# Decoder layer on one core: none of the down-projection's weight sums in the key/value stage, half of those in the up-projection through accumulating DMAs, and the down stage's activation fetches moved to another queue

## The chip, the cores and the metric

The kernel runs on one core of a Trainium2 chip. The metric is device time in microseconds (us), from the start of the program to its end, median of the runs; less is better. Engines are named as the profile names them: PE multiplies matrices (PEld loads its stationary operand), DVE is the vector engine, ACT the scalar engine, POOL and SP here mainly issue DMAs, each on a queue of its own that it works through in order.

## The reference

One layer is computed, with a sliding-window attention and a gated convolutional MLP, all in fp32, for 512 tokens of width 2048.

```
h = rms_norm(x, g[0]);  m = swa_sink_attention(h, w_in, w_out, sinks, bias_table);  x = x + rms_norm(m, g[1])
h = rms_norm(x, g[2])
u = h @ w_up                                            # 2048 x 11264
c = conv_w[0]*up[:, 0:S] + conv_w[1]*up[:, 1:S+1] + conv_w[2]*up[:, 2:S+2]    # up: u padded in front
gate, val = split(c);   y = (silu(gate) * val) @ w_down   # 5632 x 2048
x = x + rms_norm(y, g[3])
```

## The kernel before

Each fp32 matrix is split into a high part (ACT, line 64, `wh`) and a rest (DVE, line 65, `wl`), and a product is three matmuls (`prod`). A weight block is 128 x 1024 fp32, 512 KB. Split blocks go into a ring of slots (`halves`), from which PE takes them, so that PE can be a few blocks behind the splits.

Stages, in order of time: the **key/value stage** (lines 163 to 235; loop over 16 slices `kt`, each with one block of `wkv` and 24 matmuls of 512 columns, while x and its transpose are loaded); queries and attention; the output projection (`oproj` and what follows it, lines 495 to 528); the **up stage** (`up_pair(f, g)` for f = 4 to 43, line 705 on, a Strassen-like scheme with 7 products of 24 matmuls of 256 columns, so 168 matmuls, for each pair of gate and value blocks; its weight blocks are `bw`, its result goes to DRAM as `hd`); and the **down stage** (line 725 on; seven products over 22 block rows `kp`, with 88 matmuls of 512 columns and more for each four of them).

The down stage needs, beside the weights `wdn`, sums of them. They are made beforehand, in the stages above: `weight_sums(kp, sums)` loads the four blocks of a block row into four buffers `ts` (POOL's queue), adds them in place (four additions on DVE, line 144) and stores the four results to DRAM as `td` (POOL's queue again). There are 22 such block rows: before, 2 are done in the key/value stage, 6 in the output projection, 14 in the up stage. All use four `ts` buffers, so the loads of a block row wait for the stores of the one before. In the down stage `weight_form` loads a block `raw` (from `td` or `wdn`, SP's queue) and splits it; `fetch` brings `hd` back as `hq` tiles.

The order of the instructions on each engine is not that of the code: a scheduler sets it when the program is built, from its own estimate of times, and places a step where it thinks that its operands are ready. On the chip each engine then works through its list in that order. So the additions of `weight_sums` stand among DVE's splits, and where one waits for a load, the splits behind it wait too.

Of the kernel before, what the change touches and what calls it, by code (L numbers as in the profile page):

```python
# [11 lines left out]
F32 = mybir.dt.float32  # L12
F32R = mybir.dt.float32r
AF = mybir.ActivationFunctionType
ALU = mybir.AluOpType
# [3 lines left out]
P = 128  # L19
# [16 lines left out]
NP = NF // 2  # L36
# [5 lines left out]
def trunk(ctx, tc, xT, x, grow, table, onehot, masked, sinks, conv,  # L42
          wkv, wq, wo, wup, wdn, out):
    nc = tc.nc
# [93 lines left out]
    def weight_sums(kp, sums):  # L138
# [4 lines left out]
        for q, o in ((2, 0), (0, 1), (1, 2), (3, 1)):  # L143
            nc.vector.tensor_tensor(t[q], t[q], t[o], ALU.add)  # L144
            nc.gpsimd.dma_start(td[kp, :, q, :], t[q])
            yield

    def step(g, n=1):
        for _ in range(n):
            next(g, None)  # L150

    with ExitStack() as att:
# [9 lines left out]

        with ExitStack() as ph:
            pa = ph.enter_context(pool("pa", 3))
            tsk = ph.enter_context(pool("tsk", 4))

            zero = pa.tile([P, S], F32, name="zero", bufs=1)
            nc.vector.memset(zero, 0.0)
            for _ in range(2):
                mm(bank(7), zero[:, :P], zero, True, True)  # L170
            nc.scalar.activation(zero[:, 0:1], zero[:, 0:1], AF.Copy)
            first = pa.tile([P, KT + S], F32, name="first", bufs=1)
            gc = first[:, :KT]

            def token_half(b, h, ss):
                r = pa.tile([P, 1024], F32, name="xr")
                nc.sync.dma_start(r, x[b * P:(b + 1) * P, h * 1024:(h + 1) * 1024])
                nc.scalar.activation(r, r, AF.Square, accum_out=ss[:, h:h + 1])
                if h == 1:
                    nc.vector.tensor_tensor(ss[:, 0:1], ss[:, 0:1], ss[:, 1:2], ALU.add)  # L180
                    rstd(rc[:, b:b + 1], ss[:, 0:1], D, pa)

            def x_slice(kt, src):
                src = src.rearrange("p (a b) -> p a b", a=NT)
                nc.scalar.activation(ah[:, :, kt, :], src, AF.Copy, scale=gc[:, kt:kt + 1])
                nc.vector.scalar_tensor_tensor(al[:, :, kt, :], src, gc[:, kt:kt + 1],
                                               ah[:, :, kt, :].bitcast(F32), ALU.mult, ALU.subtract)

            pkv = [bank(i) for i in range(8)]
            ss = None  # L190
            for kt in range(KT):
                if kt == 0:
                    for h in range(2):
                        r = first[:, KT:] if h == 0 else pa.tile([P, 512], F32, name="xs")
                        c = KT + h * S
                        nc.sync.dma_start(r if h else first, xT[:, c if h else 0:c + S])
                        if h == 0:
                            w = halves()
                            raw = wraw.tile([P, 1024], F32, name="raw")
                            for c in (slice(0, 512), slice(512, 1024)):  # L200
                                nc.sync.dma_start(raw[:, c], wkv[0, :, c])
                                split(w[0][:, c], w[1][:, c], raw[:, c])
                        x_slice(h, r)
                elif kt % 2 == 0:
                    r = pa.tile([P, 1024], F32, name="xr")
                    nc.sync.dma_start(r, xT[:, KT + kt * S:KT + (kt + 2) * S])
                    for h in range(2):
                        x_slice(kt + h, r[:, h * 512:(h + 1) * 512])
                if kt:
                    w = weights(wkv, kt)  # L210
                if kt == 3:
                    for t, src in ((tb, table), (oh, onehot), (mk, masked)):
                        tc.keep_in_program_order(nc.sync.dma_start(t, src))
                    for e in range(2):
                        nc.sync.dma_start(sink[e * HD:(e + 1) * HD],
                                            sinks[e:e + 1].to_broadcast([HD, 2 * NKV]).rearrange("p (j g) -> p j g", g=2))
                    nc.sync.dma_start(cw, conv)
                if 4 <= kt < 12:
                    if kt % 2 == 0:
                        ss = pa.tile([P, 2], F32, name="ss")  # L220
                    token_half((kt - 4) // 2, kt % 2, ss)
                if kt == 12:
                    nc.scalar.dma_start(rd.rearrange("b p -> p b"), rc)
                    nc.scalar.dma_start(rb, rd.rearrange("b p -> (b p)")[None, :].to_broadcast([P, S]))
                for i in range(4):
                    o3 = pkv[i].rearrange("p (a b) -> p a b", a=NT)
                    prod(o3, cols(w, i), moving(kt), kt == 0, kt == KT - 1)
                if kt in (7, 11):
                    g = weight_sums(kt // 11, tsk)
                if kt >= 7:  # L230
                    step(g, (1, 0, 3, 2)[(kt - 7) % 4])
                for b in range(NT):
                    prod(pkv[4 + b], station(b, kt), wide(w, 1), kt == 0, kt == KT - 1)
            for i in range(4):
                nc.vector.tensor_tensor(kn[:, i, :], pkv[i], rb, ALU.mult)
# [209 lines left out]
    with ExitStack() as op:  # L445
# [49 lines left out]
        def oproj(d, o):  # L495
            for u in range(8):
                w = weights(wo, 8 * d + u)
                for b in range(NT):
                    for k in range(2):
                        kt = 2 * u + k  # L500
                        prod(o[b], station(b, kt), wide(w, k), kt == 0, kt == KT - 1)
                if u % 4 == 0:
                    g = weight_sums(2 * d + u // 4, sums)
                step(g, (1, 0, 2, 3)[u % 4])
            for b in range(NT):
                evac_m(b, d, o[b])
# [9 lines left out]
        for b, bk in enumerate((2, 5, 6, 7)):  # L516
            o = bank(bk)
            for kt in range(KT):
                prod(o, station(b, kt), wide(ws[kt // 2], kt % 2), kt == 0, kt == KT - 1)
                if b > 1:  # L520
                    turn_tok(b - 2, kt, (0, 1, 3, 4))
                if b < 2:
                    if kt == 0:
                        g = weight_sums(6 + b, sums)
                    if kt in (0, 9, 11, 13, 15):
                        step(g)
            evac_m(b, 3, o)
            xn[b] = finish_tok(b)
# [19 lines left out]
    batches = [(g, min(g + GB, NP)) for g in range(0, NP, GB)]  # L548
    hq = {}

    def fetch(m, par, g0, g1, queue=nc.sync):
        t, k0 = next((t, k) for t, k, k1 in hq[m, par] if k <= g0 < k1)
        queue.dma_start(t[:, g0 - k0:g1 - k0, :], hd[m, par, :, g0:g1, :])

    with ExitStack() as us:
        fp = us.enter_context(pool("fp", 1))
# [145 lines left out]
            nc.scalar.activation(uv[:, HALF:], X[:, :HALF], AF.Copy, scale=-1.0)  # L702
            gate(f, (ug, uv))

        kp, idle = 8, iter(())
        for f in range(4, NF):
            i = f - 4
            g = idle
            if kp < NP and i % 5 in (0, 2):
                work = weight_sums(kp, sums)  # L710
                step(work)
                kp += 1
            if i % 5 in (1, 4):
                g = work
            up_pair(f, g)
            step(g)
            if i == 34:
                tsu.close()
                early = ctx.enter_context(pool("early", 1, side="right"))
                hq[1, 0] = [(early.tile([P, 16, HALF], F32, name="hq10"), 0, 16)]  # L720
                for g0, g1 in batches[:4]:
                    fetch(1, 0, g0, g1)
# [13 lines left out]
    small = ctx.enter_context(pool("small3", 4))  # L736
    last = ctx.enter_context(ExitStack())
    hq[0, 0] = [(last.enter_context(pool("hq00", 1)).tile([P, NP, HALF], F32, name="hq00"), 0, NP)]
    for g0, g1 in batches[4:]:
        fetch(1, 0, g0, g1)  # L740
    for q in ((0, 0), (0, 1), (1, 1)):
        for g0, g1 in batches:
            fetch(*q, g0, g1, nc.gpsimd)
    nc.scalar.dma_start(g3, grow[2:3, :].to_broadcast([P, D]))

    XB, ZB = (3, 4, 6, 7), (0, 1, 2, 5)
# [18 lines left out]
    def weight_form(src, kp):  # L765
        raw = raws[kp % 2].tile([P, 1024], F32, name="raw")
        table, q = src
        nc.sync.dma_start(raw, td[kp, :, q, :] if table else wdn[4 * kp + q])
        hi, lo = halves()
        split(hi, lo, raw)  # L770
        return hi, lo
# [5 lines left out]
    def product(o, form, src, fresh, tail=0):  # L777
        kept = []
        for g0, g1 in batches:
            af = act_form(*form, g0, g1)  # L780
            for kp in range(g0, g1):
                wf = weight_form(src, kp)
                if kp >= NP - tail:
                    kept.append((kp, af, g0, wf))
                    continue
                for t in range(2):
                    for e in range(2):
                        multiply(o, kp, af, g0, wf, t, e, fresh)
        return kept
# [135 lines left out]
```

## Time and profile before

| | |
|---|---|
| median of 3 runs | 1944.05 us (1943.37 to 1945.49) |
| the profiled execution: its time | 1946.71 us |
| its span, first to last instruction | 1944.7 us |
| PE busy | 1876.9 us, 97% |
| DVE busy | 1492.8 us, 77% |
| ACT busy | 982.3 us, 51% |
| mean granted clock of PE | 0.982 |

The busy share of PE is high throughout, so what matters is where it is not: idle time of PE, and stretches with a lower granted clock (1.00 is 2.4 GHz, 0.50 is 1.2 GHz). The windows by stage show both.

### The profile page before, as it was taken

The page shows a single profiled execution, that of the slowest core. Times are in us where ns is not written, and L with a number is a line of the kernel's source. Part 1 is how long each engine was busy: PE and PEld are TensorE (multiplying, and loading weights), DVE is VectorE, ACT ScalarE, POOL GpSimd, SP SyncE. Part 2 cuts the span into 40 slices and gives each one's busy share as a digit, 9 for nine tenths or more (in the row PEclk, how much of TensorE's full clock was granted, in tenths as well). Part 3 has the DMA queues.
Part 4 walks back from the last instruction along what each step waited for, and adds up shares of the span by engine and source line. Part 5 has one row for each costly group of instructions (what it writes and reads, how often), then busy time and mean ns, then how long its engine had stood idle before and what let it go on. Part 6 is the DMA issues. An engine that isn't in the chain of part 4 may idle for free.

```text
span 1944.7 us, 30119 instructions
## 1 busy us (share of the span) xinstructions
PE 1876.9 (97%) x11822; PEld 1699.5 (87%) x11822; DVE 1492.8 (77%) x2079; ACT 982.3 (51%) x1566; POOL 106.1 (5%) x202
## 2 busy tenths in 40 slices
PE   8999999999999998999999999999998899999998
PEld 5878888888899998889999999999997688888886
DVE  5458888755688998999998888888886466666875
ACT  4347777632344444444455555555553455545553
POOL 2000000012100111112100000000000000000000
PEclk9999999999999999999999999999999899999999
DMA  9742333589653688788743333433333955576673
GB/s 353 208 139 81 106 113 106 184 311 327 262 182 132 234 289 269 282 298 307 254 131 114 123 123 119 137 109 120 117 119 123 343 191 192 190 237 200 218 259 118
DMA packets 116045, 375.24 MB, mean 193 GB/s; under 512 B 12704, under 2 KB 26240, under 8 KB 113984
## 3 DMA queue, kind: packets, MB, share of 16 engines
q1 hardware_dynamic: 84128, 263.19, 40.7%
q0 software_dynamic: 27744, 100.94, 14.6%
q10 hardware_dynamic: 4032, 9.21, 1.4%
q8 instruction: 92, 1.51, 0.3%
q14 instruction: 49, 0.40, 0.1%
HBM read 300.90 MB, written 72.39 MB: 192 GB/s over the span
## 4 chain that ended last, share of the span: by engine, by line
PE 67%; DMA 15%; issue 9%; DVE 7%; ACT 1%; POOL 1%; SPq 0%; DVEq 0%; ACTq 0%; POOLq 0%
PE b L83 66%; DMA td<-ts 4%; DMA ts<-in_wdn 3%; DVE wl L65 2%; DMA raw<-in_wo 2%; DMA raw<-in_wkv 1%; DMA xr<-in_x 1%; PE b L86 1%; DVE ts L144 1%; ACT wh L64 1%; DMA raw<-in_wq 1%; DMA raw<-td 1%; DMA bw<-in_wup 0%; DMA xs<-in_xT 0%; POOL ts L141 0%
## 5 line engine op out<-in xcount | busy, mean ns | idle before, releaser
L65 DVE TENSOR_TENSOR wl<-raw,wh 128x1024 fp32r<-128x1024 f32 (+1 forms) x371 | 449.1, 1218 | 240.0 <-ACT wh L64 239.3
L64 ACT ACTIVATE wh<-raw 128x1024 fp32r<-128x1024 f32 (+1 forms) x371 | 388.2, 1055 | 479.8 <-PE b L83 272.9
L83 PE MATMUL b<-ah,wl 128*128 128x256 f32 (+1 forms) x1824 | 564.5, 309 | 23.3 <-DVE wl L65 23.2
L83 PE MATMUL b<-ah,wh 128*128 128x256 f32 (+1 forms) x1824 | 570.5, 313 | 12.4 <-ACT wh L64 6.6
L83 PE MATMUL b<-al,wh 128*128 128x256 f32 (+1 forms) x1824 | 562.2, 308 | 0.4 <-DVE al L65 0.4
L83 PEld LDWEIGHTS b<-ah,wl 128*128 128x128 f32 x1824 | 356.4, 195 | 41.8 <-DVE wl L65 26.9
L83 PEld LDWEIGHTS b<-ah,wh 128*128 128x128 f32 x1824 | 356.4, 195 | 27.5 <-ACT wh L64 10.3
L83 PEld LDWEIGHTS b<-al,wh 128*128 128x128 f32 x1824 | 356.7, 196 | 11.1 <-DVE al L65 0.6
L83 PE MATMUL b<-wh 128*128 128x512 f32 x616 | 241.1, 391 | 18.5 <-ACT wh L64 18.0
L83 PE MATMUL b<-wl,wh 128*128 128x512 f32 x616 | 240.8, 391 | 0.5 <-DVE wl L65 0.5
L83 PE MATMUL b<-wh,wl 128*128 128x512 f32 x616 | 240.6, 391 | 0.0
L64 ACT ACTIVATE wh<-bw 128x1024 fp32r<-128x1024 f32 x160 | 167.7, 1055 | 129.7 <-PE b L83 129.7
L65 DVE TENSOR_TENSOR wl<-bw,wh 128x1024 fp32r<-128x1024 f32 x160 | 194.5, 1219 | 9.7 <-ACT wh L64 9.3
L83 PEld LDWEIGHTS b<-wh 128*128 128x128 f32 x616 | 116.3, 189 | 43.4 <-ACT wh L64 18.4
L83 PEld LDWEIGHTS b<-wl,wh 128*128 128x128 f32 x616 | 116.3, 189 | 25.2 <-DVE wl L65 1.0
L144 DVE TENSOR_TENSOR ts<-ts 128x1024 f32<-128x1024 f32 x88 | 107.4, 1220 | 39.3 <-DMA ts<-in_wdn 35.7
L83 PEld LDWEIGHTS b<-wh,wl 128*128 128x128 f32 x616 | 116.2, 189 | 24.1
L83 PE MATMUL b<-wh,ah 128*128 128x512 f32 x320 | 126.9, 397 | 0.0
L83 PE MATMUL b<-wl,ah 128*128 128x512 f32 x320 | 124.9, 390 | 0.2 <-DVE wl L65 0.2
L83 PE MATMUL b<-wh,al 128*128 128x512 f32 x320 | 124.9, 390 | 0.0
L670 ACT ACTIVATE s<-b 128x256 f32<-128x256 f32 x160 | 59.2, 370 | 90.2 <-PE b L83 90.2
L83 PE MATMUL b<-f5h,wl 128*128 128x256 f32 x320 | 90.9, 284 | 2.2 <-DVE wl L65 2.2
(162 smaller groups left out, 3063.7 us busy)
## 6 DMA issues: line engine op xcount, KB each, us to landing
bw<-in_wup SPq DMA_DIRECT2D x160, 512.0 KB, 3.8
ts<-in_wdn POOLq DMA_DIRECT2D x88, 512.0 KB, 7.3
td<-ts POOLq DMA_DIRECT2D x88, 512.0 KB, 5.8
raw<-td SPq DMA_DIRECT2D x88, 512.0 KB, 4.8
raw<-in_wdn SPq DMA_DIRECT2D x66, 512.0 KB, 4.3
raw<-in_wq SPq DMA_DIRECT2D x32, 512.0 KB, 3.5
raw<-in_wo SPq DMA_DIRECT2D x32, 512.0 KB, 4.6
hd<-c SPq DMA_DIRECT2D x44, 256.0 KB, 3.1
```

The costliest lines, as they stand in the source:

```text
L64: nc.scalar.activation(hi, src, AF.Copy)
L65: nc.vector.tensor_tensor(lo, src, hi.bitcast(F32), ALU.subtract)
L83: tc.keep_in_program_order(nc.tensor.matmul(o, l, r, start=start, stop=stop, skip_group_check=more))
L86: tc.keep_in_program_order(nc.tensor.transpose(o, src, ident))
L144: nc.vector.tensor_tensor(t[q], t[q], t[o], ALU.add)
L670: nc.scalar.activation(t, o[:, :HALF], AF.Copy)
```

## The change

In the key/value stage the two block rows of sums are gone; the output projection takes block rows 0 to 5 instead of 2 to 7. The up stage takes 16 instead of 14: of every five pairs the first starts a `weight_sums` as before, the second runs its additions and then calls `queue_sums`, a new function that makes the same four results without DVE: a load, then a second DMA on POOL's queue that adds its source into the buffer (`accum_op=ALU.add`), then the store. In the down stage the fetches of `hq` that POOL's queue issued at its start are put on SP's queue, in the code one for every two weight blocks.

```diff
+    def queue_sums(kp, sums):
+        t = [sums.tile([P, 1024], F32, name="ts") for _ in range(4)]
+        for q, other in ((2, 0), (0, 1), (1, 2), (3, 1)):
+            nc.gpsimd.dma_start(t[q], wdn[4 * kp + q])
+            nc.gpsimd.dma_start(t[q], wdn[4 * kp + other] if q in (0, 2) else t[other], accum_op=ALU.add)
+            nc.gpsimd.dma_start(td[kp, :, q, :], t[q])
...
-            tsk = ph.enter_context(pool("tsk", 4))
...
-                if kt in (7, 11):
-                    g = weight_sums(kt // 11, tsk)
-                if kt >= 7:
-                    step(g, (1, 0, 3, 2)[(kt - 7) % 4])
...
-                    g = weight_sums(2 * d + u // 4, sums)
+                    g = weight_sums(2 * d - 2 + u // 4, sums)
...
-                        g = weight_sums(6 + b, sums)
+                        g = weight_sums(4 + b, sums)
...
-    def fetch(m, par, g0, g1, queue=nc.sync):
+    def fetch(m, par, g0, g1):
...
-        queue.dma_start(t[:, g0 - k0:g1 - k0, :], hd[m, par, :, g0:g1, :])
+        nc.sync.dma_start(t[:, g0 - k0:g1 - k0, :], hd[m, par, :, g0:g1, :])
...
-        kp, idle = 8, iter(())
+        kp = 6
         for f in range(4, NF):
             i = f - 4
-            g = idle
-            if kp < NP and i % 5 in (0, 2):
+            if i % 5 == 0 and kp < NP:
                 work = weight_sums(kp, sums)
                 step(work)
                 kp += 1
-            if i % 5 in (1, 4):
-                g = work
-            up_pair(f, g)
-            step(g)
-            if i == 34:
+            up_pair(f, work if i % 5 == 1 else iter(()))
+            if i % 5 == 1:
+                step(work)
+            if i % 5 == 1 and kp < NP:
+                queue_sums(kp, sums)
+                kp += 1
+            if kp == NP and tsu:
                 tsu.close()
...
-    for g0, g1 in batches[4:]:
-        fetch(1, 0, g0, g1)
-    for q in ((0, 0), (0, 1), (1, 1)):
-        for g0, g1 in batches:
-            fetch(*q, g0, g1, nc.gpsimd)
+    coming = [(1, 0, *g) for g in batches[4:]] + [(*q, *g) for q in ((0, 0), (0, 1), (1, 1)) for g in batches]
...
                 wf = weight_form(src, kp)
+                if coming and kp % 2 == 0:
+                    fetch(*coming.pop(0))
```

What the scheduler makes of it stands in the orders. POOL's queue in the up stage, before: one block row of sums (buffers `ts_6433` to `ts_6436`; `td<-ts` are the stores, which also wait for DVE's additions):

```order
L141 DMA ts_6433<-in_wdn 128x1024
L141 DMA ts_6435<-in_wdn 128x1024
L145 DMA td_89<-ts_5946 128x1024
L141 DMA ts_6434<-in_wdn 128x1024
L141 DMA ts_6436<-in_wdn 128x1024
L145 DMA td_89<-ts_6435 128x1024
L145 DMA td_89<-ts_6433 128x1024
```

The same queue after the change, from the fifth `queue_sums` on (`ts_8831` to `ts_8834`; line 151 loads, line 152 adds, line 153 stores; lines 141 and 145 belong to the `weight_sums` ahead of it):

```order
L151 DMA ts_8833<-in_wdn 128x1024
L145 DMA td_89<-ts_8342 128x1024
L151 DMA ts_8831<-in_wdn 128x1024
L152 DMA ts_8833<-in_wdn 128x1024
L145 DMA td_89<-ts_8344 128x1024
L151 DMA ts_8832<-in_wdn 128x1024
L152 DMA ts_8831<-in_wdn 128x1024
L153 DMA td_89<-ts_8833 128x1024
L151 DMA ts_8834<-in_wdn 128x1024
L152 DMA ts_8832<-ts_8833 128x1024
L153 DMA td_89<-ts_8831 128x1024
L152 DMA ts_8834<-ts_8832 128x1024
```

The store of the last sum follows in the next row but two, behind two loads of the next `weight_sums`. On DVE the additions stood from the 4th pair of the stage to the 16th, four of them for each 0.9 pairs; after the change they stand in eight groups of four, one group for each 2.4 pairs, from the 4th pair's gate to the 21st's (32 additions in 17.4 pairs).

SP's queue at the start of the down stage, before (`hd<-c` are the last results of the up stage, `raw` the weight blocks kp 0, 2, 4, 6 and then 1, 3, 5 and on, `hq10b` the last part of one activation quarter; the other 18 fetches stand on POOL's queue):

```order
L768 DMA raw<-td 128x1024
L576 DMA hd<-c_15413 128x2x256
L768 DMA raw<-td 128x1024 x2
L576 DMA hd<-c_15650 128x2x256
L553 DMA hq10b<-hd 128x1024
L553 DMA hq10b<-hd 128x512
L768 DMA raw<-td 128x1024 x18
```

And after:

```order
L768 DMA raw<-td 128x1024 x2
L555 DMA hq_15683<-hd 128x1024 x2
L578 DMA hd<-c_15646 128x2x256
L555 DMA hq_15683<-hd 128x1024 x3
L555 DMA hq_15683<-hd 128x512
L555 DMA hq10b<-hd 128x1024
L768 DMA raw<-td 128x1024
L555 DMA hq10b<-hd 128x512
L768 DMA raw<-td 128x1024
L555 DMA hq_15675<-hd 128x1024 x5
L555 DMA hq_15675<-hd 128x512
L555 DMA hq_15676<-hd 128x1024 x5
```

All 18 fetches that POOL's queue had are on SP's queue ahead of the seventh weight block, kp 5: the first six ahead of kp 1, the other twelve between kp 3 and kp 5.

## Rows read from the trace of the kernel before

**Rows 1.** Windows, whole core: span; PE, PEld, DVE, ACT, POOL busy (count); clock; DMA share; GB/s.

```profile
0.00:50.00 50.00, 40.52 (x138) 28.27 (x139) 26.44 (x39) 23.92 (x35) 11.16 (x24) 0.93 0.97 355
...
450.00:500.00 50.00, 50.00 (x222) 41.42 (x221) 30.25 (x29) 15.67 (x26) 11.77 (x22) 1.00 0.90 326
...
800.00:850.00 50.00, 44.12 (x337) 43.30 (x336) 44.49 (x49) 20.81 (x30) 9.59 (x18) 0.93 0.81 286
...
1000.00:1050.00 50.00, 50.00 (x419) 50.00 (x419) 43.38 (x48) 26.05 (x37) 0.00 (x0) 1.00 0.39 127
...
1500.00:1550.00 50.00, 33.55 (x134) 27.15 (x135) 22.66 (x19) 17.66 (x18) 8.55 (x17) 0.80 0.94 349
```

**Rows 2.** PE's timeline, key/value stage: its first and its last matmul (start us, us).

```profile
5.64 0.80 PE L83 MATMUL b<-ah,wh 128*128 128x512 f32 x1
...
106.64 0.39 PE L83 MATMUL b<-wh,al 128*128 128x512 f32 x1
```

**Rows 3.** DMA, 0 to 70 us: all packets; then one issue (count, KB, median us to landing).

```profile
DMA packets 7626, 23.43 MB, mean 335 GB/s; under 512 B 1520, under 2 KB 1712, under 8 KB 7622
ts<-in_wdn POOLq DMA_DIRECT2D x8, 512.0 KB, 9.6
```

**Rows 4.** PE's timeline, up stage: the last product (f4h) of pairs f = 4, 19, 20.

```profile
658.75 0.28 PE L83 MATMUL b<-f4h,wh 128*128 128x256 f32 x1
...
1007.61 0.28 PE L83 MATMUL b<-f4h,wh 128*128 128x256 f32 x1
...
1027.77 0.28 PE L83 MATMUL b<-f4h,wh 128*128 128x256 f32 x1
```

**Rows 5.** DVE, 645 to 960 us: the additions (duration min/median/max ns), and its waits (us, times, longest).

```profile
L144 DVE TENSOR_TENSOR ts<-ts x56: 1207/1218/1228, 655.4 to 948.1; 128x1024 f32<-128x1024 f32 x56
...
DVE ts L144 <- DMA ts<-in_wdn: 15.6, 9, 2.9
DVE raw L679 <- DMA bw<-in_wup: 8.5, 4, 3.7
```

**Rows 6.** DMA, 650 to 960 us, up stage with sums.

```profile
DMA packets 27305, 90.22 MB, mean 291 GB/s; under 512 B 2843, under 2 KB 6171, under 8 KB 27281
q0 software_dynamic: 15981, 58.18, 54.4%
td<-ts POOLq DMA_DIRECT2D x56, 512.0 KB, 6.0
ts<-in_wdn POOLq DMA_DIRECT2D x52, 512.0 KB, 6.3
```

**Rows 7.** DMA, 400 to 520 us, output projection with sums.

```profile
DMA packets 10402, 39.99 MB, mean 333 GB/s; under 512 B 1168, under 2 KB 1168, under 8 KB 9883
td<-ts POOLq DMA_DIRECT2D x24, 512.0 KB, 4.6
ts<-in_wdn POOLq DMA_DIRECT2D x23, 512.0 KB, 7.7
```

**Rows 8.** The tile ts, 645 to 960 us: issue duration in ns; us to landing.

```profile
L141 POOL DMA_DIRECT2D ts<-in_wdn x56: 527/532/549, 646.6 to 938.0; - x56
...
DMA to landing us min/median/max: 2.9/6.2/11.4
```

**Rows 9.** Chain that ended last, start of the down stage (start us, us, what); then PE's wait there.

```profile
1503.92 10.88 DMA raw<-td
...
1517.24 27.77 PE b L83 x110
...
PE b L83 <- ACT wh L64: 18.0, 1, 18.0
```

**Rows 10.** Windows of 2.5 us there, columns as in the first group.

```profile
1497.50:1500.00 2.50, 0.48 (x3) 0.06 (x1) 1.44 (x2) 0.00 (x0) 1.01 (x2) 1.00 0.55 186
...
1507.50:1510.00 2.50, 0.00 (x0) 0.00 (x0) 0.00 (x0) 0.00 (x0) 0.53 (x1) 0.50 1.03 415
...
1522.50:1525.00 2.50, 2.50 (x12) 2.02 (x11) 0.00 (x0) 1.04 (x1) 0.54 (x1) 0.97 1.03 411
```

More of the change, by code (lines that the diff above doesn't have):

```diff
@@ L712, in trunk @@
                 kp += 1
-            if i % 5 in (1, 4):
-                g = work
-            up_pair(f, g)
-            step(g)
-            if i == 34:
+            up_pair(f, work if i % 5 == 1 else iter(()))
[5 more added lines that the diff above has]
+            if kp == NP and tsu:
                 tsu.close()
+                tsu = None
                 early = ctx.enter_context(pool("early", 1, side="right"))
```

## Prediction, made before the change was run

> **What bounds the kernel now.** I read the windows first, since PE is busy 97% of the whole span and an average tells little. In [rows 1] the reader is to see where PE's busy time is short of the window or its clock below 1.00: the first 50 us, the up stage while sums are made (44.12 of 50 at a clock of 0.93), and the start of the down stage (33.55 of 50 at 0.80). The output projection makes sums too, with DMA at 0.90, and PE has no gap. After the sums, from 1000 us on, PE is full and DVE has 43.38 of 50.
>
> Three losses of PE follow, each with its cause.
>
> The key/value stage: its 384 matmuls run from 5.64 to 106.64 us [rows 2], 101.0 us. At the spacing of a full window (50 us for 222, so 0.226 us each [rows 1]) they need 383 x 0.226 = 86.6 us. The loss is 14.4 us. DMA is at 0.97 of its time there [rows 1]; 23.43 MB are moved in the first 70 us [rows 3], of which the sums are 8 loads and 8 stores of 0.524 MB, 8.4 MB, more than a third.
>
> The up stage: the last product of pair 4 begins at 658.75, that of pair 19 at 1007.61, that of pair 20 at 1027.77 [rows 4]. A free pair takes 20.16 us; the 15 pairs took 348.9 where 302.4 were needed. The loss is 46.4 us, half of it clock. The cause is DVE: 56 additions of 1.22 us, 68 us, and 24 us in which it stood before loads [rows 5]. A free pair leaves DVE 20.16 - 20.16 x 43.38/50 = 2.67 us, over 15 pairs 40 us. 68 + 24 - 40 = 52, against 46.4 measured: the account is right to about 6 us, and high.
>
> The down stage's start: PE waits 18.0 us for one split, that of the weight block kp 1, issued at 1503.92 and landed 10.88 us later [rows 9], and the clock is at 0.50 in and after the gap [rows 10]: some 21 us.
>
> **The change part by part.**
>
> Key/value stage. 8.4 MB of 23.4 and 8 additions go. What is left, 15 MB, would take 45 us at the 335 GB/s of [rows 3], half of PE's 87, so DMA is no longer late except in the first blocks. Of 14.4 us I leave 3 for these and the first matmuls: **-11**. Bounds: -14 (nothing is late) and -7 (half of the loss lies in the first three blocks, which wait for their own loads).
>
> Output projection. Six block rows as before, only others: 0. The cover is PE's full windows [rows 1]; were it gone, DVE's lag would cost at most what a sum costs in the up stage, 46.4/14 = 3.3 us each, and their number is the same.
>
> Up stage. Two things have to keep pace with PE. First DVE: 32 additions are 39 us, and by its order they stand over 17.4 pairs, where 17.4 x 2.67 = 46 us are free. Waits for loads were 24/14 = 1.7 us a sum; eight sums make 14 us. 39 + 14 - 46 = 7 us lost. The additions come in groups of four, 4.9 us within some 0.7 pairs that have 1.9 us free: 3 us too much in each of 8 groups, 24 us if PE had no blocks in hand, 0 if its ring covers all. I take 9.
>
> Second POOL's queue. Let L be a load, S a store and A an adding DMA, from issue to landing. Following the queue in the order shown: the last addition lands (A); its store (S) frees the buffer for the fourth load of the next `weight_sums`; behind that load stands the store of its first result (S), which frees the buffer for the first load of the next `queue_sums` (L); then its first addition (A), the one that uses it (A), and the last again. With seven issues of 0.53 us [rows 8] the round is 3A + 2S + L + 3.9. DVE's order gives it 2.41 pairs, 48.5 us. With S = 6.0 and L = 6.3 [rows 6] A may be 8.8; with 4.6 and 7.7, at 333 GB/s [rows 7], 9.2. The second is the better row, because a round at that pace moves 20 x 0.524 MB of sums and 2.41 x 2.36 MB of the pairs' own, 334 GB/s. If a round is longer, additions on DVE wait for their loads, the splits behind them wait, and PE with them, seven times.
>
> No row has an adding DMA. Nearest below is the load at 6.3 [rows 6]: a round of 41 us, nothing lost. Nearest above, if everything but the smallest landing of 2.9 us [rows 8] doubles: 2 x 7.7 - 2.9 = 12.5, a round of 58. I take 9.2, the load at this traffic plus one more transfer of its bytes, an estimate: POOL's queue moved 58.18 MB in 54.4% of 310 us [rows 6], 1.5 us for 0.524 MB. That is a round of 48 to 50, and I put down 5 us. Sum: 7 + 9 + 5 = 21 lost instead of 46: **-25**. Bounds: -42 (the round of 41 us and every group of additions covered by the ring), and +39 (the second rival, below).
>
> The Trainium skill has a rule that speaks against this part: "Collectives: The Full Stack", section "The bandwidth ceiling: the fold count and why AG ≠ RS ≠ AR", says that an add in the DMA path needs two source reads on the same ring, so that it moves data at half the rate of a copy. No run here shows it. By it, if it applied only to the transfer, the sum stays as above; if to all of the time under load, it is the second rival's.
>
> The early fetch of `hq` on SP's queue waits for all sums. Its place is behind the weight loads of pair 25, and the sums end some two pairs after DVE's last addition (3A + 2S + 3 = 40 us by the same walk), near pair 23: 0. Queued behind it are the weights of pairs 26 and on; it would cost PE only with rounds so long that the second rival has them priced.
>
> Down stage. In the code a fetch comes with every second weight block; in SP's order it doesn't. Six fetches of hq_15683 and one of hq10b stand ahead of kp 1, twelve more between kp 3 and kp 5. Kp 1: from 1497 to 1504 some 3.6 MB are issued on one queue and at the 415 GB/s of [rows 10] 2.9 MB of it are moved, so kp 1 has 0.7 and its own 0.5 MB to wait for, and lands near 1510 instead of 1514.8: -5. Kp 5: 6.3 MB behind kp 3, 15 us, lands near 1528, split by 1530; PE, with kp 1 to 4 done, wants it near 1526: +4, and perhaps 2 of clock. **0**, between -8 and +8.
>
> **Sum.** -11 - 25 + 0 = -36. The profiled execution has a span of 1944.7 us and a time of 1946.71, 0.14% over the median of 1944.05; the differences are taken from the median: **1908**.
>
> **The rivals.**
>
> The gain of the up stage is eaten: adding DMAs take about 10.7 us, the round is 53 us, 4.5 x 7 = 31 more are lost, 16 + 31 = 47, what was lost before. Only the key/value stage is left: 1933. For it: landings of 7.7 to 9.6 us at the same traffic [rows 3, 7]. Against it: additions between two buffers don't read DRAM.
>
> Slower, by one mechanism: the queue of POOL is the bound of the up stage, because an adding DMA occupies the DMA engines twice. A = 12.5, a round of 58.3 us against 48.5, 9.8 x 7 = 69 on top of 16: 85 us lost, 39 more than before; less 11, **1972**. It decides from A = 11.2 on, where the total is nought: 16 + 7 x 3 x (A - 9.2) = 46 + 11. For it: the round is a chain of six landings, and nothing of it overlaps. Against it: the 1.5 us of transfer in a landing of 6 to 8 us.
>
> The change doesn't do what it says: the fetches stand together in SP's order. This is certain already and costs 0, as above; its bad end, kp 5 late and the clock down for longer, is +8: 1916, which lies in the forecast's range.
>
> **How the numbers follow.** The forecast (1890 to 1920) has 0.50, the first rival 0.20 for a faster end (1920 to 1940) and 0.05 for one within 0.2% (3.9 us, about what a measurement can tell from no change), the second rival 0.22, better than 1890 0.03. Faster 0.73, same 0.05, slower 0.22. The range has the first rival and the second to just over its price, and leaves out some 0.1 above (A beyond 12.7) and little below: 1885 to 1975.
>
> **What would show it.** Right: the key/value stage's last matmul near 96 us; the pairs from 4 to 21 near 21.3 us each; adding DMAs landing in 8 to 10 us; DVE's waits for `ts` loads below 20 us in the up stage; kp 1 landing earlier and a second short gap at kp 5. Wrong: adding DMAs over 11 us, with POOL waiting for them and DVE before `ts` loads in every round, pairs at 23 us and more until the 21st, PE's clock at 0.50 again and again; or DVE full in these pairs without waits, so that the groups of additions cost more than 9 us.

## The result, and the profile of the changed kernel

The changed kernel takes 1919.23 us (median of 1915.05, 1916.24, 1922.22 and 1922.58) against 1943.88 for the kernel before on the same chip: a ratio of 0.987, 95% interval 0.985 to 0.990, 25 us faster. Run a second time on another chip it gave 0.985 (0.982 to 0.988). The forecast was 1908 with a range of 1885 to 1975: right in direction and in the sign of both gains, and 11 us too low.

The profiled execution has a span of 1913.3 us and is the fastest of the four; before's, 1944.7, was slower than its median. So the profiles differ by 31.4 us where the medians differ by 24.7. What follows adds up the profiles.

The windows that answer to [rows 1], same columns:

```profile
0.00:50.00 50.00, 48.49 (x196) 37.45 (x197) 29.14 (x54) 35.56 (x52) 2.47 (x8) 1.00 0.88 304
450.00:500.00 50.00, 50.00 (x223) 41.38 (x222) 27.62 (x31) 12.24 (x19) 11.21 (x21) 1.00 0.91 341
800.00:850.00 50.00, 48.53 (x400) 47.92 (x400) 41.30 (x47) 25.95 (x38) 12.24 (x20) 1.00 0.94 303
900.00:950.00 50.00, 44.11 (x340) 43.30 (x340) 41.16 (x45) 22.59 (x32) 12.21 (x20) 0.93 0.98 324
1000.00:1050.00 50.00, 48.52 (x404) 48.31 (x404) 45.43 (x50) 24.06 (x36) 10.38 (x17) 1.00 0.98 311
1450.00:1500.00 50.00, 28.85 (x140) 23.62 (x139) 18.79 (x20) 13.76 (x17) 0.00 (x0) 0.79 0.83 310
```

The key/value stage is nearly full now and the output projection still is. The up stage is better than before at 800, but not free, and it still makes sums at 1000, where before had none; the DMA share is the figure that changed most there, 0.94 to 0.98 against 0.81. The start of the down stage still has its hole.

PE's waits from 0 to 130 us, of before and then of after (us, times, longest):

```profile
PE b L83 <- ACT wh L64: 5.3, 3, 3.1
PE b L83 <- DVE wl L65: 2.7, 4, 1.4
PE b L83 <- DVE kn L235: 2.6, 1, 2.6
PE b L83 <- DVE zero L168: 1.5, 1, 1.5
```

```profile
PE b L83 <- DVE zero L174: 1.5, 1, 1.5
```

Every wait but the warm-up's is gone. The timeline of PE has the stage's first matmul at 5.52 and its last at 93.51; then, in the up stage, the last product of pairs 4, 19, 21 and 43 (to hold against [rows 2, 4]):

```profile
5.52 0.79 PE L83 MATMUL b<-ah,wh 128*128 128x512 f32 x1
...
93.51 0.39 PE L83 MATMUL b<-wh,al 128*128 128x512 f32 x1
...
641.17 0.28 PE L83 MATMUL b<-f4h,wh 128*128 128x256 f32 x1
...
967.88 0.28 PE L83 MATMUL b<-f4h,wh 128*128 128x256 f32 x1
...
1009.54 0.28 PE L83 MATMUL b<-f4h,wh 128*128 128x256 f32 x1
...
1455.40 0.28 PE L83 MATMUL b<-f4h,wh 128*128 128x256 f32 x1
```

The 15 pairs from 4 to 19 take 326.7 us where they took 348.9, and the 17 from 4 to 21 take 21.7 us each.

Three lengths are read from such rows, for every kernel below: the time of **pair 4**; the **up loss**, from pair 4 to pair 43 less 39 x 20.16 = 786.2 us; and the **tail**, from pair 43 to the end of the span. Before: 658.8, 832.6 - 786.2 = 46.4, 453.3. After: 641.2, 814.2 - 786.2 = 28.0, 457.9. The differences, -17.6, -18.4 and +4.6, are the 31.4 us. Of the up loss of 28.0 us, 18.6 are idle time of PE and the rest is a lower clock, a mean of 0.98 from pair 4 to 21.

DVE's waits from 640 to 1080 us, the stretch with sums (us, times, longest), and its additions there (duration min/median/max in ns, first and last start):

```profile
L144 DVE TENSOR_TENSOR ts<-ts x31: 1208/1219/1227, 640.2 to 1016.3; 128x1024 f32<-128x1024 f32 x31
```

```profile
DVE raw L681 <- DMA bw<-in_wup: 17.0, 11, 3.5
DVE bw L692 <- DMA bw<-in_wup: 10.8, 5, 3.2
DVE wl L65 <- ACT wh L64: 8.9, 12, 1.7
DVE ts L144 <- DMA ts<-in_wdn: 8.9, 4, 2.7
DVE ts L144 <- DMA td<-ts: 7.9, 1, 7.9
```

The additions are as short and as few as forecast. The waits for transfers are 17.0 + 10.8 + 8.9 + 7.9 = 44.6 us, of which 27.8 are for `bw`, the pairs' own weights, and not for the sums. But the longest single wait is for `ts`, and so are others where PE loses most. Pairs 7 and 17 (last products near 709 and 925 us) take 27.5 and 28.5 us, so 15.7 us are lost in these two, and DVE stands before additions in both (start us, us, what, idle before it and for what):

```profile
687.51 1.22 DVE L144 TENSOR_TENSOR ts<-ts 128x1024 f32<-128x1024 f32 x1 [7.87 <-DMA td<-ts]
...
900.53 1.23 DVE L144 TENSOR_TENSOR ts<-ts 128x1024 f32<-128x1024 f32 x1 [2.54 <-DMA ts<-in_wdn]
...
906.27 1.23 DVE L144 TENSOR_TENSOR ts<-ts 128x1024 f32<-128x1024 f32 x1 [2.71 <-DMA ts<-in_wdn]
```

The DMA of the same stretch (queue's packets, MB, share of 16 engines; issues with KB each and median us to landing), beside [rows 6]:

```profile
DMA packets 40288, 132.25 MB, mean 301 GB/s; under 512 B 4193, under 2 KB 9393, under 8 KB 40251
q0 software_dynamic: 22475, 81.83, 60.8%
q1 hardware_dynamic: 17776, 49.91, 31.5%
bw<-in_wup SPq DMA_DIRECT2D x82, 512.0 KB, 7.0
ts<-in_wdn POOLq DMA_DIRECT2D x76, 512.0 KB, 8.3
td<-ts POOLq DMA_DIRECT2D x63, 512.0 KB, 6.3
ts<-ts POOLq DMA_DIRECT2D x16, 512.0 KB, 8.5
```

The adding DMAs between two buffers land in 8.5 us. The loads, at 8.3 with the other adding DMAs among them, and the pairs' `bw` at 7.0 are slow as well: the engines are busy 92% of the stretch.

PE's waits in the tail, after (before had one of 18.0, [rows 9]):

```profile
PE b L83 <- ACT wh L64: 19.4, 2, 15.4
```

### The profile page after: what moved, and what is told of

Same layout as the page of the kernel before. It is cut to its first block, busy times and chain, and to the rows that moved or that the text cites. A ratio compares the mean times of both kernels' runs of the same rounds, so it can differ in the third digit from the quotient of the medians.

```text
span 1913.3 us, 30053 instructions
## 1 busy us (share of the span) xinstructions
PE 1862.9 (97%) x11822; PEld 1689.4 (88%) x11822; DVE 1455.1 (76%) x2047; ACT 980.9 (51%) x1566; POOL 125.9 (7%) x216
## 4 chain that ended last, share of the span: by engine, by line
PE 68%; DMA 16%; issue 9%; DVE 6%; ACT 1%; POOL 1%; DVEq 0%; SPq 0%; ACTq 0%; POOLq 0%
PE b L83 66%; DMA ts<-in_wdn 4%; DMA bw<-in_wup 3%; DMA ts<-ts 2%; DVE wl L65 2%; DMA raw<-in_wo 2%; PE b L86 1%; DMA td<-ts 1%; ACT wh L64 1%; DVE ts L144 1%; DMA hq<-hd 1%; DMA raw<-td 0%; DMA raw<-in_wup 0%; DVE xt L482 0%; DVE c L569 0%
## 5 line engine op out<-in xcount | busy, mean ns | idle before, releaser
L83 PE MATMUL b<-ah,wh 128*128 128x256 f32 (+1 forms) x1824 | 561.9, 308 | 0.9 <-ACT s L672 0.5
L83 PE MATMUL b<-ah,wl 128*128 128x256 f32 (+1 forms) x1824 | 555.8, 305 | 5.9 <-DVE wl L65 5.9
L83 PE MATMUL b<-al,wh 128*128 128x256 f32 (+1 forms) x1824 | 554.4, 304 | 0.4 <-DVE al L65 0.4
L83 PEld LDWEIGHTS b<-ah,wl 128*128 128x128 f32 x1824 | 348.8, 191 | 22.3 <-DVE wl L65 7.7
L83 PEld LDWEIGHTS b<-ah,wh 128*128 128x128 f32 x1824 | 349.3, 192 | 13.2 <-ACT wh L64 2.0
L83 PEld LDWEIGHTS b<-al,wh 128*128 128x128 f32 x1824 | 349.4, 192 | 11.0 <-DVE al L65 0.6
L144 DVE TENSOR_TENSOR ts<-ts 128x1024 f32<-128x1024 f32 x56 | 68.4, 1221 | 40.2 <-DMA ts<-in_wdn 31.8
L83 PE MATMUL b<-f6h,wh 128*128 128x256 f32 x320 | 92.3, 288 | 5.0 <-ACT s L672 5.0
```

Of the source, the lines that this page charges most:

```text
L83: tc.keep_in_program_order(nc.tensor.matmul(o, l, r, start=start, stop=stop, skip_group_check=more))
```

## The experiments

All ratios are to the kernel before on the same chip. Pair 4, up loss and tail come from the profiled execution of each; the execution behind the median can differ by some us.

| kernel | us | ratio, 95% | pair 4 | up loss | tail |
|---|---|---|---|---|---|
| after | 1919.2 | 0.987 (0.985 to 0.990) | 641.2 | 28.0 | 457.9 |
| after_again | 1917.0 | 0.985 (0.982 to 0.988) | 640.7 | 30.5 | 459.4 |
| kv_only | 1923.6 | 0.991 (0.988 to 0.993) | 641.6 | 42.3 | 452.3 |
| up_only | 1930.4 | 0.995 (0.992 to 0.997) | 658.5 | 34.4 | 452.7 |
| fetch_pool | 1913.0 | 0.986 (0.984 to 0.988) | 641.1 | 31.1 | 451.7 |
| fetch_pinned | 1909.7 | 0.982 (0.979 to 0.984) | 642.4 | 27.8 | 450.2 |
| plain_load | 1899.0 | 0.979 (0.977 to 0.981) | 641.6 | 8.9 | 459.7 |
| no_dve_adds | 1888.6 | 0.972 (0.969 to 0.974) | 641.1 | 0.1 | 459.2 |
| spread | 1904.0 | 0.979 (0.976 to 0.982) | 642.4 | 28.4 | 449.9 |
| dram_sums | 1967.2 | 1.012 (1.009 to 1.016) | 730.0 | 0.0 | 448.6 |
| queue_all | 1891.4 | 0.973 (0.969 to 0.976) | 642.1 | 8.3 | 449.9 |
| best | 1885.1 | 0.970 (0.967 to 0.972) | 641.6 | 10.7 | 444.8 |

### One part at a time

`kv_only`, the kernel before with

```diff
-                if kt in (7, 11):
-                    g = weight_sums(kt // 11, tsk)
-                if kt >= 7:
-                    step(g, (1, 0, 3, 2)[(kt - 7) % 4])
...
-        nc.sync.dma_start(raw, td[kp, :, q, :] if table else wdn[4 * kp + q])
+        nc.sync.dma_start(raw, td[kp, :, q, :] if table and kp > 1 else wdn[4 * kp + q])
```

> The kernel before with the two sums of the key/value stage left out: the down stage reads plain weight blocks for kp 0 and 1 in their place, so this run leaves those sums out of the computation and is read for its time alone; the other 20 sums, the queues and the fetches are as before. Theory of the prediction: the stage gives back 11 us and nothing else moves, 1933 us. Theory from the trace after: the stage gives back 13 to 14 us, and the change of stage behind it another 4 (the wait for kn and the clock after it), so that pair 4's last product comes 17.5 us earlier, near 641, and the time is near 1926.5. Rival: the gain is taken back later, because the up stage or the down stage comes earlier against its own transfers: pair 4 at 641 but a time above 1930.

Measured: 16.8 us below before, pair 4 at 641.6, tail unchanged. The trace's theory holds. The gain isn't taken back.

`up_only`, the kernel before with `queue_sums` and the changed kernel's loop over the pairs, from kp 8 on.

> The kernel before with only the up stage changed: 14 sums, seven by DVE and seven by adding DMAs, in seven rounds; key/value stage and fetches as before. Theory of the prediction: seven rounds lose 5 of 7 plus 9 and 6, some 18 to 21 us against 46, so -25, 1919 us. Theory from the trace after (28 us lost in eight rounds, 3.5 a round): 24.5 lost in seven rounds, -22, 1922. Rival: the up stage of the changed kernel gained only because it had been reached with other work ahead of it; then less than 15 us are gained, 1929 or more.

Measured: 10.1 us below before (a ratio of 0.992 to 0.997 is 6 to 15 us); its executions spread from 1924 to 1934. That is under both theories' forecasts, and the rival's number came, less than 15 us and above 1929. Its reason did not, since the parts add up: on this chip 16.8 + 10.1 = 26.9, and `fetch_pool`, which has both and no other, is 27.5 below before. So the up stage's change is worth 10 to 18 us, depending on the execution, not 25.

`fetch_pool`, the changed kernel with the 18 fetches on POOL's queue as before.

> The changed kernel with the fetches of hq for the down stage put back on POOL's queue where they stood before. Theory of the prediction: 0, between -8 and +8, so 1919. Theory from the trace after: the 4.7 us that the stage from the up stage's end on lost come from the fetches on SP's queue ahead of kp 1 and kp 5, so the time is near 1914.5 and the start of the down stage has one gap of some 18 us at kp 1. Rival: with the sums ending two pairs later and the fetches on the queue of the sums, nothing changes: 1919.

Measured: a ratio within the error of the changed kernel's, so the times alone don't tell. The tails do. The four kernels with the fetches on POOL's queue (before, `kv_only`, `up_only`, `fetch_pool`) have 451.7 to 453.3, the four with them together on SP's (after, `after_again`, `plain_load`, `no_dve_adds`) 457.9 to 459.7. By the tails, of one execution each, the place on SP's queue costs 5 to 8 us; the two ratios, 0.987 and 0.986, give about 3.

`after_again`, the changed kernel itself.

> The changed kernel itself, once more, beside the two that follow: 24 to 26 us below the kernel before on the same chip, near 1919. If its ratio stands more than 0.3% off 0.987, the differences between runs of other chips are less certain than they look.

Measured: as expected, 0.985. Ratios on different chips agree to 0.2%.

### What the adding DMA costs, and who pays

`plain_load`, the changed kernel with

```diff
-            nc.gpsimd.dma_start(t[q], wdn[4 * kp + other] if q in (0, 2) else t[other], accum_op=ALU.add)
+            nc.gpsimd.dma_start(t[q], wdn[4 * kp + other] if q in (0, 2) else t[other])
```

> The changed kernel with each adding DMA made a plain transfer of the same bytes between the same places: half of the up stage's sums are left out of the computation. It gives the price of adding by itself. Theory A (an add costs little over a load, and the rounds of 52.6 us are long because all landings under this traffic are, 8.3 us): landings at 8 us or more still, rounds of 50 to 52 us, time within 4 us of 1919. Theory B (an add occupies the DMA engines for two reads): landings of the former adds fall below 7 us, rounds to 45 to 48 us, the two stalls of 7 us go and the time is 1903 to 1909.

Measured: 1899, up loss 8.9; theory B in its main point: the two stalls go (pairs 7 and 17 take 20.2 and 21.6 us), and more is gained than it had. Its rounds of 45 to 48 us did not come. They take 49.0, which is DVE's pace of 2.41 pairs. Its DMA from 640 to 1080 us and DVE's waits there:

```profile
q0 software_dynamic: 22486, 81.86, 50.6%
bw<-in_wup SPq DMA_DIRECT2D x86, 512.0 KB, 6.3
ts<-ts POOLq DMA_DIRECT2D x16, 512.0 KB, 7.0
```

```profile
DVE raw L681 <- DMA bw<-in_wup: 11.9, 6, 3.3
DVE ts L144 <- DMA ts<-in_wdn: 6.3, 3, 2.6
```

The bytes of q0 are the same to 0.1%, the engines' share is 50.6% and not 60.8%. A plain transfer of 0.524 MB takes 0.506 x 440 / (81.86 / 0.524) = 1.43 us of all 16 engines; the 32 adding DMAs take 0.102 x 440 / 32 = 1.40 us more each, 2.83: twice as long. That the engines are fuller doesn't explain it: the packets of q1, all plain, take 1.46 us for 0.524 MB in the changed kernel and 1.48 here. The landing hardly shows it, 8.5 against 7.0, and the other landings grow too, `bw` from 6.3 to 7.0. It shows in everybody's waits: DVE's for transfers are 18.2 us here and 44.6 in the changed kernel.

`no_dve_adds`, the changed kernel with the additions of `weight_sums` left out in the up stage.

> The changed kernel without DVE's 32 additions in the up stage, which leaves half of that stage's sums out of the computation; loads, adding DMAs and stores remain. The prediction's account gave DVE 7 + 9 = 16 us of the loss. By it the up stage's loss falls from 28 to 32 to 12 to 16 and the time to some 1903. Theory O (the DMA engines' time is what is short): the loss falls by less than 8 us, 1911 to 1919.

Measured: 1888.6, up loss 0.1: neither theory, and more than either forecast. A window of it, as above, its `bw` loads from 640 to 1080 us, its adding DMAs between buffers (first and last start) and DVE's largest wait for transfers:

```profile
800.00:850.00 50.00, 50.00 (x419) 50.00 (x418) 42.98 (x49) 27.71 (x40) 12.22 (x20) 1.00 0.99 324
```

```profile
bw<-in_wup SPq DMA_DIRECT2D x87, 512.0 KB, 7.5
```

```profile
L153 POOL DMA_DIRECT2D ts<-ts x16: 867/889/917, 662.8 to 1009.9; - x16
```

```profile
DVE bw L693 <- DMA bw<-in_wup: 2.5, 2, 1.7
```

The engines are as full as they get and the landings longer than in the changed kernel, and PE loses nothing. So full engines cost nothing here by themselves. In the changed kernel they cost through DVE, which has to take the `bw` and `ts` loads in its order. The run takes two things from DVE at once, the 39 us of additions and the places at which it stood before `ts` loads and stores; no run parts the two.

The last adding DMAs of the rounds start from 672.24 to 1009.92 here, 48.2 us apart, so POOL's queue keeps the 48.5 us of DVE's order when DVE doesn't hold it up. With plain transfers and DVE's additions the round takes 49.0, with both 52.6. What is lost isn't a sum of two prices: adding DMAs without DVE's additions lose 0.1 us, the additions without adding lose 8.9 (`plain_load`), both together 28.0.

The prediction's own account, additions + waits - 46 us that the pairs leave free, can be redone with the waits that were measured: after 39 + 45 - 46 = 38 (up loss 28.0), `after_again`, with waits of 49.2, 42 (30.5), `plain_load` 39 + 18 - 46 = 11 (8.9), `no_dve_adds` 5 - 46, nothing (0.1). But the 46 belong to the 17.4 pairs of the additions and the waits to 640 to 1080 us, some 20 pairs, which leave 54 free; with these the account gives 30, 34, 3 and nothing. So it puts these runs in the right order and is good to about 10 us.

`queue_all`, the `fetch_pinned` kernel (below) with the other half of the sums made by adding DMAs too:

```diff
-            if i % 5 == 0 and kp < NP:
-                work = weight_sums(kp, sums)
...
+            up_pair(f, iter(()))
+            if i % 2 == 0 and kp < NP:
                 queue_sums(kp, sums)
                 kp += 1
-            if kp == NP and tsu:
+            if i == 36:
...
-                    fetch(1, 0, g0, g1)
+                    fetch(1, 0, g0, g1, nc.gpsimd)
...
```

> The fetch_pinned kernel with all 16 sums of the up stage made by adding DMAs: none is left for DVE, 32 more adding DMAs go through the engines, which have to be at their full share for some 25 pairs; the early fetch of hq goes to POOL's queue so that it waits behind the sums without holding SP's. Theory V (the up stage loses what DVE lacks: 39 us of additions and 44 us of waits for loads against some 54 us that the pairs leave it free): without the additions DVE has 54 us for 44 us or somewhat more of waits, the up stage loses 0 to 4 us, and the time is 26 to 30 us below fetch_pinned, 1880 to 1885. Theory O (the loss follows the share of the DMA engines): 32 adding DMAs more, each twice a load, lose more than the 28 us of now: above 1910.

Measured: 1891.4, 0.009 of before or 18 us below `fetch_pinned`, where 26 to 30 were expected. Theory O falls: 32 adding DMAs more, and the up stage loses 8.3 us where `fetch_pinned` lost 27.8. Theory V holds in direction; 8.3 us remain where it had 0 to 4. Its queue, DVE's waits and PE's, 640 to 1080 us:

```profile
q0 software_dynamic: 23881, 86.95, 69.6%
```

```profile
DVE bw L692 <- DMA bw<-in_wup: 28.2, 12, 3.9
DVE raw L681 <- DMA bw<-in_wup: 9.7, 11, 2.5
```

```profile
PE b L83 <- ACT s L672: 5.4, 4, 2.2
```

DVE waits longer for `bw` than in the changed kernel, 37.9 us, and has the time for it except in three or four pairs. The account has nothing left there, so the 8.3 us stay open; single late loads are a guess. They do show that full engines aren't always free for a DVE with time to spare.

### Pace and place

`spread`, the `fetch_pinned` kernel with DVE's additions held at their place in the code and a round every four pairs:

```diff
-            nc.vector.tensor_tensor(t[q], t[q], t[o], ALU.add)
+            tc.keep_in_program_order(nc.vector.tensor_tensor(t[q], t[q], t[o], ALU.add))
...
-            if i % 5 == 0 and kp < NP:
+            if i % 4 == 0 and kp < NP:
...
```

> The fetch_pinned kernel with each of DVE's additions of sums held behind what the code puts before it, and a round every four pairs: the same loads, adds and stores, over 32 pairs instead of some 19. Theory O (the DMA engines are too full while the sums last, since an adding DMA takes them twice as long as a load, 2.8 us against 1.4): the same work over 32 pairs leaves them under 0.75, the up stage loses under 8 us instead of 28 to 32, the time is 20 to 25 us below fetch_pinned. Theory C (the chain of landings on POOL's queue in a round, or the groups of four additions on DVE, cost their price wherever they stand): eight rounds still lose 20 us or more, and the time is within 8 us of fetch_pinned.

Measured: 1904.0, up loss 28.4 in the profiled execution, which is the slowest of the four (1908.7); by the numbers, theory C. But the trace shows another reason for nearly half of it. From pair 35 to pair 36 it takes 33.1 us. SP's waits there, 1270 to 1330 us, and DVE's:

```profile
SPq L555 <- DMA td<-ts: 14.5, 2, 11.2
```

```profile
1297.25 1.23 DVE L681 TENSOR_TENSOR raw<-bw 128x1024 f32<-128x1024 f32 x1 [13.11 <-DMA bw<-in_wup]
```

The early fetch of `hq` (L555) waits for the last sums, and SP's queue with the pairs' loads waits behind it: the trap that the prediction looked for at pair 25 and put at 0, since the sums there end in time. Without these 13 us some 15 are left, in five stalls of 2 to 6 us. So spreading helps less than theory O said, and neither is clean; a spread kernel without that fetch on SP's queue wasn't tried.

`dram_sums`, the `fetch_pinned` kernel with the up stage's sums made in the attention stage, from DRAM to DRAM:

```diff
+    def dram_sums(kps):
+        for kp in kps:
+            for q in range(4):
+                tc.keep_in_program_order(nc.gpsimd.dma_start(td[kp, :, q, :], wdn[4 * kp + q]))
+        for q, other in ((2, 0), (0, 1), (1, None), (3, None)):
+            for kp in kps:
+                src = td[kp, :, 2 if q == 1 else 1, :] if other is None else wdn[4 * kp + other]
+                tc.keep_in_program_order(nc.gpsimd.dma_start(td[kp, :, q, :], src, accum_op=ALU.add))
...
+        for k in range(0, 16, 2):
+            dram_sums((6 + k, 7 + k))
...
```

> The fetch_pinned kernel with the 16 sums of the up stage moved into the attention stage and made there in DRAM alone: per row of td a transfer from wdn and one adding DMA, 8 for a kp, none through SBUF. In the attention stage the DMA engines have a share of 0.30 to 0.47 and DVE 42 of 50 us. Theory: an adding DMA counts twice for the engines, so 16 x (4 + 4 x 2) x 1.43 = 275 us of the engines in a stage of some 290 us of which they have 190 free: the sums last to about 530 us, through the output projection, whose own sums and loads they delay; the up stage is free of sums, its 28 us go, and 0 to 10 us are lost in attention and output projection: 18 to 28 below fetch_pinned. Rival: the reads of DRAM and the full engines make wq and wo late, PE waits in the attention stage, and more than 28 us are lost there: above fetch_pinned.

Measured: 1967.2; the rival. The up stage is clean, but pair 4 comes at 730.0, 88 us late. PE's waits from 330 to 620 us, and the DMA from 100 to 400:

```profile
PE b L83 <- DMA ah<-od: 40.7, 3, 23.0
PE b L83 <- DMA al<-od: 10.2, 1, 10.2
```

```profile
q0 software_dynamic: 14503, 52.80, 73.8%
ah<-od SPq DMA_DIRECT2D x3, 1024.0 KB, 33.0
```

The reloads of the attention's output land in 33.0 us, where they took 9.9 in the changed kernel, and PE waits 50.9 us for them. The rest of the 88 us is smaller waits and the clock, at 0.69 and 0.76 in the two windows from 350 to 450 us. Room in an average share of 0.3 is no room for a transfer that is needed at once.

### The start of the down stage

`fetch_pinned`, the changed kernel with

```diff
-        nc.sync.dma_start(t[:, g0 - k0:g1 - k0, :], hd[m, par, :, g0:g1, :])
+        tc.keep_in_program_order(nc.sync.dma_start(t[:, g0 - k0:g1 - k0, :], hd[m, par, :, g0:g1, :]))
```

> The changed kernel with the fetches of hq held in the code's order on SP's queue, one behind the weight block of every second kp, so that kp 1 has two of them ahead of it and not seven. From the last f4h product to the end the changed kernel takes 457.9 us, the one with the fetches on POOL's queue 451.7, the kernel before 453.3. Theory: the place of the fetches on SP's queue costs these 5 to 6 us, and the 18 us gap at kp 1 is theirs as well; then that stretch falls to 436 to 448 us and the time to 1897 to 1909. Rival: the start of the down stage is bound by the bytes that have to come there, in whatever order; then 452 to 458 remain, 1913 to 1919.

Measured: 1909.7, tail 450.2: the 5 to 8 us come back and a little more, but 436 to 448 was expected, and the gap at kp 1 stays, 15.6 us. The first half of the theory holds, the second falls. SP's timeline (start us, us, what):

```profile
1463.26 0.80 SPq L555 DMA_DIRECT2D hq<-hd  x2
1464.15 0.38 SPq L578 DMA_DIRECT2D hd<-c  x1
1471.52 0.32 SPq L555 DMA_DIRECT2D hq10b<-hd  x1
1471.88 0.43 SPq L768 DMA_DIRECT2D raw<-td  x1
```

Kp 1 (the last row) isn't late for the bytes ahead of it. It stands behind the fetch of hq10b, which waits 6.9 us for the last pair's store of `hd` to land.

`best`, the `queue_all` kernel with

```diff
-        raw = raws[kp % 2].tile([P, 1024], F32, name="raw")
         table, q = src
+        raw = raws[0 if q == 2 and kp < 4 else kp % 2].tile([P, 1024], F32, name="raw")
```

> The queue_all kernel with the first four weight blocks of the down stage all loaded through wraw, whose memory is free early, in place of every second one through wraw2, whose memory the up stage still holds. In fetch_pinned kp 1 waits on SP's queue behind the fetch of hq10b, which waits 6.9 us for the last store of hd, and PE stands 15.6 us. Theory: kp 0 to 3 are split before the up stage ends, their 18 us of matmuls cover that, the gap and most of the low clock behind it go: 12 to 18 us below queue_all. Rival: kp 4 or 5 is late in their place, since their loads stand behind the same fetch and the engines are full there: 0 to 6 us below.

Measured: 1885.1, 6 us below `queue_all` with intervals that overlap, and a tail of 444.8, 5 us shorter: the rival. PE's wait is 5.5 us and not 15.7. It beats both kernels of the case: 60 us, 3%, below before, 1.5% below the changed one by the ratios on that chip.

## Why the prediction was right in direction and 11 us off

**Key/value stage**, -11 between -14 and -7: the stage went from 101.0 to 88.0 us, -13, near "nothing is late", so the 3 us left for the first blocks were 1. Another 4.6 went where the prediction had no term: PE's wait of 2.6 for `kn` and the lower clock behind it, 0.71 from 110 to 115 us, between this stage and the next, vanished too. Measured -17.6, 6 or 7 too little.

**Output projection**, 0: right, PE full in its window.

**Up stage**, -25: this is the step that failed, with -18.4 in the profiled execution and -10.1 by the medians of `up_only`. Term by term:

- DVE's account, 7: the additions were sized right, 39 us, the free time too. The waits weren't. Fourteen us were put down, 1.7 for each of eight sums, as if they belonged to the sums and were halved with them. They were 44.6, 27.8 of them before `bw`; without adding they are 18.2 (`plain_load`), so most of them come with the adding DMAs.
- The groups of four, 9: the account with measured waits, 30 to 38, reaches the loss without them, and no run shows them apart. The two DVE terms together, 16, stand against the 8.9 us that `plain_load` loses.
- POOL's round, 5: this is the term that was too small. What is lost more with adding than without is 28.0 - 8.9 = 19.1 us. A was taken as 9.2 and measured 8.5, within the 8 to 10 of "what would show it", and S as 4.6, measured 6.3, L as 7.7, measured 8.3; with these the prediction's formula gives a round of 50.3. The last adding DMA of a round comes every 52.6 us (675.0 to 1043, seven rounds), not 48 to 50. The mechanism, an addition that waits and the splits and PE behind it, is seen in pairs 7 and 17, 15.7 us in two rounds and not a little in each of seven.

The prediction held the cause of this and used it in the wrong place. It asked whether an adding DMA that occupies the engines twice would land at 12.5 us. It occupies them twice, 2.83 us against 1.43, and lands at 8.5. The Trainium skill, "Collectives: The Full Stack", section "The bandwidth ceiling: the fold count and why AG ≠ RS ≠ AR", explains why ReduceScatter, a collective operation, has half the rate of a copy by an add that needs two source reads. That is said of collectives only; for the engines' time of these DMAs the runs agree, 1.98 times, for the landing they don't. What had to be added up was the engines' time in a round: 16 plain transfers of 1.43 and 4 adding ones of 2.83 are 34 us, the pairs' own 31.5% of 52.6 are 17, together 51 us. This is some 3 us high, since the engines do it in 48.2 where nothing holds the queue (`no_dve_adds`); but that is all of the 48.5 us that DVE's order gave it, and leaves no time in which POOL waits for DVE or DVE for a load. The second rival's mechanism was there, its price of 1972 wasn't. The first rival's round of 53 us was there, at A = 8.5 and not 10.7; its price, 4.5 us in each of seven rounds, wasn't, and the up stage kept a gain.

**Early fetch**, 0: right here; in `spread` the same fetch, later sums ahead of it, cost 13 us.

**Down stage**, 0 between -8 and +8: +4.6. The mechanism was as written: PE's first wait 15.4 instead of 18.0, a second of 4.0 at kp 5, both in the row of the tail's waits above. Kp 1 was issued at 1469.59, 14.2 us after pair 43's product (before: 12.5), behind hq10b; the gain of 5 at kp 1 was 2.6, the second wait takes it back, and the clock falls a second time (0.57 from 1495 to 1500 us). That is the way in which the third rival, the fetches standing together, had its bad end at +8.

The terms as measured, -17.6 - 18.4 + 4.6, against -11 - 25 + 0: a sum of -31 for -36 in the profiles, and -25 by the medians. The two differ since before's profiled execution was 2.8 us above its median and the changed kernel's 4.2 below. Luck had a part in how near the total came: the 6 or 7 us too little for the key/value stage made up for as much of the up stage's 7 to 15 too many, and 1919 is 1 us inside the 1890 to 1920 that the prediction gave to its forecast.

Of its signs, these came: pairs at 21.7 us each (21.3), adding DMAs at 8.5 us (8 to 10), DVE's waits before `ts` at 16.8 us (below 20), the second gap at kp 5. The key/value stage ended at 93.5 and not near 96. Two slips in its sums move nothing: seven issues of 0.53 us are 3.7 and not 3.9, and the bound of -42 should be -39 while the 7 us of DVE's account stay.

## What to carry to other kernels

When work moves to a busy DMA system, add up the engines' time per round beside the latency of the chain: an accumulating DMA counted as two transfers here although its landing hardly showed it. Late transfers cost most where the engine that takes them in order has no slack, and a queue and an engine that nearly keep the pace alone lose far more once they wait for each other (0.1 and 8.9 us, together 28.0). So give the work to whichever of the two, that engine or the queues, still has some: here moving all the sums off DVE was worth more than moving half, although it filled the DMA engines completely. A transfer on a queue can wait for something far away, and whatever stands behind it waits too: look for that at every move, at the place where it ends up and not where the code has it.

## What the runs showed of the hardware

An adding DMA of 0.524 MB takes 2.83 us of the 16 engines where a plain one takes 1.43, and lands 1.5 us later (8.5 and 7.0). POOL takes 0.897 us to issue it between two buffers, 0.532 for a plain one; the changed kernel's rows and then `plain_load`'s (duration min/median/max in ns):

```profile
L152 POOL DMA_DIRECT2D ts<-ts x16: 882/897/914, 663.7 to 1042.9; - x16
```

```profile
L152 POOL DMA_DIRECT2D ts<-ts x16: 527/532/542, 663.9 to 1015.1; - x16
```

The engines at a share of 0.99 to 1.03 for 350 us didn't slow a PE that was fed through an engine with slack (`no_dve_adds`, up loss 0.1); at that share for 500 us, with 32 adding DMAs more, 8.3 us were lost (`queue_all`). And adding DMAs work from DRAM to DRAM at the same cost: in `dram_sums` q0 moved 52.80 MB in 73.8% of 300 us, 2.20 us for 0.524 MB, near the mean of 1.43 and 2.83.
